# Mixer outputs of a two-layer encoder trunk: gated projections by seven half-size products, weight sums by accumulating transfers

## The chip, the cores and the metric

The kernel runs on one core of one Trainium2 chip. The metric is the device time of one execution in microseconds. Each time is the median of several runs of the same program; one more execution is recorded by the hardware profiler, and its trace has its own time. Engines: PE (TensorE) multiplies matrices, DVE (VectorE) and ACT (ScalarE) do elementwise work, POOL (GpSimd) issues some DMAs and does small elementwise work, SP (SyncE) issues the weight loads.

## The reference

Two layers over 640 tokens (512 of a prompt and 8 x 16 of running streams) with a width of 1024:

```python
x += 0.5 * swiglu_1(rmsnorm(x))
z = rmsnorm(x) @ w_in            # columns: B | C | V | q | k | v | gates (2 x 1024)
g_conv, g_attn = split(sigmoid(z_gates + b_gate))
y_conv = B * causal_depthwise_conv3(C * V)          # 512 channels
y_attn = chunk_band_attention(q, k, v)              # 8 heads x 64
m = g_conv * (y_conv @ w_conv_out) + g_attn * (y_attn @ w_attn_out)
x += m @ w_o
x += 0.5 * swiglu_2(rmsnorm(x))
```

All data are fp32. The change is in the line that computes m: `y_conv @ w_conv_out` and `y_attn @ w_attn_out`, each 512 channels in and 1024 columns out, each result multiplied by its gate, the two summed.

## The kernel before, in words

**Layout.** Activations are kept transposed: tiles of 128 channels by 640 tokens. x has 8 such tiles, y_conv and y_attn 4 each, the mixture m 8 ("mixtures" below are these tiles, m_0 to m_7). Tokens fall into two halves of 320, written t1 and t2.

**Precision.** Each fp32 operand is split into a high part (rounded to the fp32r format, a cast on ACT) and a low part (operand minus high part, a subtraction on DVE). A product is three matmuls of 128 x 128 weights with 320 tokens: high x high, high x low, low x high. So every slab of weights costs an ACT cast (whi) and a DVE subtraction (wlo).

**Weights.** All weights lie in HBM in the order of their use, in slabs of 128 x 1024 (512 KB). SP loads them into a ring of three raw tiles (`load`, L275). `source` (L293) says which columns make up the next piece, `prep` (L334) casts it on ACT and notes the subtraction, `flush` (L350) issues noted subtractions on DVE, `slab` (L357) takes the next piece and prepares the piece after the next, `quiet` (L378) takes one without preparing, and `ahead` (L370) issues the load and sums of a piece in advance.

**Plain products and products by seven.** A plain product of one output tile is 4 input tiles x 2 token halves x 3 = 24 matmuls (`product`, L432; for the output products of w_o it is 8 input tiles, 48 matmuls). Most of the kernel computes two output tiles at a time by seven products in place of eight: the 2 x 2 blocks are (output tile, token half) by (even and odd input tile). A unit takes two slabs of weights, from which four pieces of 1024 columns (the last of 512) are made by sums on DVE (four adds of 512 columns, two of which can be replaced by lent sums, below), and seven mixed operands of the inputs, called X11, X21, N6, T5, T7, X22, T4. Each of the seven is a block of 12 matmuls (`block`, L436), in the order of their names. X11, N6, T7 and T4 accumulate one after the other in accumulator pa, X21 in pb, T5 and X22 in pc. ACT copies pa out after X11 (to c1) and after N6 (to u2), and pc after T5 (to c5), before the next block goes on in the same accumulator. DVE adds these copies to the results.

**Stage around the change.** `outputs` (L1469) runs after attention. Its engines' order is the order in which the code issues instructions (PE, DVE and ACT; POOL and SP are ordered by a scheduler). `gate_pair` (L1479) computes two tiles of gates by seven, 84 matmuls, and applies the sigmoid (L1334) at its end. `out` (L1522) computes one projection tile by a plain product (accumulator py, one of two) and multiplies it by its gate (L1530, L1532), for the attention branch adding it to the mixture. The order is given by `mixer_order` (L114): gates 2 and 3, projections 0 to 3 of y_conv, then six times a pair of gates followed by two projections. `take` (L1538) splits y into parts ahead of its products, `give` (L1542) splits the finished mixtures m_0 to m_7, which take the place of the normed input in memory (tiles hhi and hlo). After that come the eight output products po of `mixer` (about L1408 to L1418), each over all eight mixtures, added to x.

**Lent sums.** In the FFN the seven-product units on the list LEAN get one weight sum not from DVE but from two DMAs on POOL's queue: the first copies 128 x 512 weights into a tile, the second adds other weights onto it (`lend`, L268; transfers L272 and L273). The second waits for the first. In the mixers there are none.

Of the kernel before, what the change touches and what calls it, by code (L numbers as in the profile page):

```python
# [57 lines left out]
ROWS = (1, 2)  # L58

MARGIN = 2, 4  # L60
LEAN = {"a0": (1, 6), "b0": (1, 5), "a1": (0, 5), "b1": (1, 5)}

XT4, XN6, XT7, X21, X22, X11, XT5 = range(7)
# [64 lines left out]


# [6 lines left out]
def stages():  # L136

    out, done = [], []

    def end(kind):  # L140
        done.append((kind, out[:]))
        out.clear()

    def plain(n):
        out.extend([8] * (n // 8) + [n % 8] * (n % 8 > 0))

    def ffn(name):
        held = 0
        for what, a in ffn_order(name):
            if what == "gu":  # L150
                plain(held)
                held = 0
                out.append("gu")
            elif what == "std":
                held += 2 * KT
            elif what == "cut":
                plain(held)
                held = 0
            elif what == "rows":
                plain(held)  # L160
                held = 0
                out.append("gu")
            elif what == "ends":
                held += KT * len(a)
            else:
                held += sum(len(js) for _, js in a)
        plain(held)

    for l in range(L):
        ffn(f"a{l}")  # L170
        end("ffn")
        held = 0
        for what, _ in mixer_order():
            if what == "mix":
# [12 lines left out]
def two(ps):  # L187
    return ps[:, :, :HT]
# [7 lines left out]
def trunk(ctx: ExitStack, tc: tile.TileContext, xin, wst, small, pbias, samplebias, kcache, vcache, gfin,  # L196
# [54 lines left out]
    for kind, units in stages():  # L251
        n = sum(2 if z in ("gu", "mix") else 1 for z in units)
        if kind == "ffn":
            inner.update(range(at + MARGIN[0], at + n - MARGIN[1]))
        at += n
    raws, ready = [], []
    sums, pool, spool = {}, [None], [None]
    lent, lean, at = {}, set(), 0
    for name, (_, units) in zip([f"{k}{l}" for l in range(L) for k in "amb"], stages()):
        ns = []  # L260
        for z in units:
            if z == "gu":
                ns.append(at)
            at += 2 if z in ("gu", "mix") else 1
        if name in LEAN:
            lean.update(ns[slice(*LEAN[name])])
# [26 lines left out]
    def source(i):  # L293

        if i >= len(slabs):
            return None
        if i not in sources:
            kind, n, arg = slabs[i]
            ra = load(n)
            if kind == "plain":  # L300
                sources[i] = [(ra, slice(0, arg))]
            elif arg == 0:
                if n in lean and n not in lent:
                    lend(n)
                sources[i] = [(ra, whole)]
            else:
                rb = load(n + 1)
                if arg == 1 and kind == "gu":
                    if n + 2 in lean:
                        lend(n + 2)  # L310
                    st = sums[n] = pool[0].tile([P, CH], F32, tag="s65", name=f"s65_{n}", bufs=1)
                    add(st[:, h2], rb[:, h1], rb[:, h2])
                    add(st[:, h1], st[:, h2], ra[:, h1])
                    sources[i] = [(st, whole)]
                elif arg == 1:

                    flush()
                    st = sums[n] = spool[0].tile([P, CH // 2], F32, tag="s6", name=f"s6_{n}", bufs=1)
                    add(ra[:, h1], ra[:, h1], rb[:, h1])
                    add(st, ra[:, h1], rb[:, h2])  # L320
                    add(rb[:, h1], rb[:, h1], rb[:, h2])
                    sources[i] = [(st, h1), (rb, h1)]
                elif arg == 2:
                    if kind == "gu" and n not in lean:
                        add(ra[:, h1], ra[:, h1], rb[:, h1])
                    add(ra[:, h2], sums.pop(n)[:, h1], ra[:, h2])
                    sources[i] = [(lent.pop(n), h1), (ra, h2)] if n in lean else [(ra, whole)]
                else:
                    sources[i] = [(rb, h2)]
        return sources[i]  # L330

    pending = []
# [984 lines left out]
    def mixer(l, after):  # L1317
        with tc.tile_pool(name=f"yp{l}", bufs=1, reuse_waits="tile") as yp, \
# [84 lines left out]
            with tc.tile_pool(name=f"gp{l}", bufs=1, reuse_waits="tile") as gp, \  # L1403
                 tc.manual_schedule(engines=ORDERED):
                hold[0] = True
                mo = outputs(l, gp, ops.X, st, cs, ycs, yas, sigmoid, gates)
        ex = after()
        with tc.manual_schedule(engines=ORDERED):  # L1408
            hold[0] = True
            for m in range(KT):  # L1410
                po = acc(f"po{l}_{m}")
                product(po, mo)
# [53 lines left out]
        def t5(self, kp):  # L1466
            self.parts(*(z[:, HT:] for z in self.h[2 * kp]), self.a[kp][:, 1])

    def outputs(l, gp, X, st, cs, ycs, yas, sigmoid, gates):  # L1469
# [4 lines left out]
        mm = ycs + [spare[i // 2][:, i % 2] for i in range(CT)]  # L1474
# [4 lines left out]
        def gate_pair(m, then=None):  # L1479
# [5 lines left out]
            ACT.copy(c1, pa)  # L1485
# [7 lines left out]
            ACT.copy(u2, pa)  # L1493
            block(pc, s1, 1, XT5, every, True, True)
            ACT.copy(c5, pc)
            s2 = slab(True)[0]
# [5 lines left out]
            if then:  # L1502
                then()
            block(pc, s2, 1, X22, every, False, True)
            add(u[:, t2], pc, u2)
            s3 = slab(True)[0]
            DVE.tensor_tensor(out=u, in0=u, in1=rr, op=ALU.mult)
# [6 lines left out]
            sigmoid(g, m + 1, -1.0)  # L1514
            flush()

        def parts(pool, tag, name, src):
# [3 lines left out]

        def out(m, y, then=None):  # L1522

            py = acc(f"py{l}_{m}")
            product(py, y)
            if then:
# [7 lines left out]
            flush()  # L1534

        yc, ya, mo = [], [], []

        def take(y, name, srcs):  # L1538
            for c, src in enumerate(srcs):
                y.append(parts(gp, f"y{c}", f"{name}{l}_{c}", src))  # L1540
# [5 lines left out]
        gate_pair(2, lambda: take(yc, "yc", ycs))  # L1546
        for m in range(4):
            out(m, yc)
        for m in range(4, 2 * KT, 2):
            last = m == 2 * KT - 2  # L1550
            gate_pair(m, (lambda: take(ya, "ya", [yas[:, c, :] for c in range(CT)])) if m == KT else
                      (lambda: give(range(1))) if last else None)
            y = yc if m < KT else ya
            out(m, y, (lambda: give(range(1, 4))) if last else None)
            out(m + 1, y, (lambda: give(range(4, 6))) if last else None)
        give(range(6, KT))
        return mo

    def attention(l, h, norms, stats, ops, mp, yas, ycp, both, others):
# [517 lines left out]
def _stream(i):  # L2077
# [9 lines left out]
    for l in range(L):  # L2087
# [36 lines left out]
        for what, m in mixer_order():  # L2124
            if what == "v":
                out.append(v.reshape(KT // 2, 2, P, AW).transpose(0, 2, 1, 3).reshape(-1, P, CH))
            elif what == "mix":
                out.append(chunks(held))
                held = []

                out.append(chunks([rows[name][a][o::2] for name, a in m for o in range(2)]))
            else:
                held.append(rows[what][m])
        out.append(chunks(held))
# [71 lines left out]
```

## Time and profile before

| | |
|---|---|
| median of 3 runs | 2489.51 us (2488.77 to 2489.75) |
| the profiled execution's own time | 2488.93 us |
| span in its trace | 2487.1 us |
| mean granted TensorE clock | 0.999 |
| weight loads on SP | 375 of 512 KB |
| lent sums on POOL | 36 transfers of 256 KB |

In the page and the views of the trace, "busy" counts the time in which an engine has an instruction running. Matmuls overlap, so a matmul's duration is not what it costs; the distance between starts is. Instructions of DVE and ACT overlap a little too. A group line gives the operation, the tiles written and read, the shapes, the count, busy time and mean duration in ns, and then the idle time of the engine before these instructions with what ended it. A timeline line gives start, duration, engine, line, operation, tiles, and in brackets the idle time before it. A window line gives, for a stretch of the span, the busy time of each engine with its instructions, the granted clock, the busy share of the DMA engines and GB/s.

### The profile page before, as it was taken

Reading aid. Unit: us, or ns where it says so; the run is one execution under the profiler, and the core shown is the slowest. Engines: PE = TensorE matmul, PEld = TensorE weight load, DVE = VectorE, ACT = ScalarE, POOL = GpSimd, SP = SyncE. Lnnn points to the kernel's source line nnn. Section 1 sums busy time; section 2 is a strip of 40 time slices with the busy share of each in tenths; the row PEclk is TensorE's granted clock in tenths of the full one; section 3 lists DMA queues with packets and bytes.
Section 4 is the critical chain, followed back from the end, with each engine's and each line's share of the span. In section 5 each row is a group of like instructions: output and inputs, shape, how many; then the busy total and the mean of one; then the engine's idle time right before and its main releaser. Section 6 shows DMA issues by size and latency. Waiting matters only on the chain.

```text
span 2487.1 us, 43918 instructions
## 1 busy us (share of the span) xinstructions
PE 2473.8 (99%) x17312; PEld 2421.2 (97%) x17312; DVE 2140.1 (86%) x3533; ACT 1355.4 (54%) x2152; POOL 298.4 (12%) x451
## 2 busy tenths in 40 slices
PE   9999999999999999999999999999999999999999
PEld 8999999889999999999999999998999999999998
DVE  7999998888776899998799999988886769999997
ACT  6555556665444655555665555556644455555555
POOL 0111112211000001111001011121110000111111
PEclk9999999999999999999999999999999999999999
DMA  4443545335223333444334443453442232444444
GB/s 155 126 118 101 124 118 121 113 108 174 77 82 114 93 102 105 113 117 117 111 93 109 110 118 101 116 128 106 133 157 86 77 111 87 109 116 105 113 117 117
DMA packets 109934, 279.75 MB, mean 112 GB/s; under 512 B 12480, under 2 KB 52032, under 8 KB 109728
## 3 DMA queue, kind: packets, MB, share of 16 engines
q1 hardware_dynamic: 69552, 220.10, 28.0%
q0 software_dynamic: 39744, 56.60, 12.3%
q8 instruction: 135, 2.21, 0.4%
q14 instruction: 71, 0.58, 0.1%
q10 hardware_dynamic: 432, 0.25, 0.0%
HBM read 231.09 MB, written 7.94 MB: 96 GB/s over the span
## 4 chain that ended last, share of the span: by engine, by line
PE 94%; DVE 3%; ACT 2%; issue 1%; DMA 1%; SPq 0%; DVEq 0%; ACTq 0%; POOLq 0%
PE pab L442 12%; PE paa L442 11%; PE pcb L442 6%; PE daa L1127 6%; PE pca L442 5%; PE dab L1127 5%; PE po L418 5%; PE py L418 5%; PE qa L442 4%; PE pbb L442 3%; PE dca L1127 3%; PE pba L442 3%; PE dcb L1127 2%; PE ma_cv L442 2%; PE ma_qk L442 2%; PE pv L1612 2%
## 5 line engine op out<-in xcount | busy, mean ns | idle before, releaser
L352 DVE TENSOR_TENSOR wlo<-raw,whi 128x1024 fp32r<-128x1024 f32 (+1 forms) x569 | 579.9, 1021 | 155.9 <-ACT whi L347 152.8
L347 ACT CAST whi<-raw 128x1024 fp32r<-128x1024 f32 (+1 forms) x569 | 504.7, 890 | 380.1 <-PE pbb L442 47.2
L347 ACT CAST whi<-s 128x1024 fp32r<-128x1024 f32 (+1 forms) x158 | 150.3, 951 | 296.1 <-issue 111.2
L442 PE MATMUL pab<-xhib,whi 128*128 128x320 f32 x704 | 217.7, 309 | 0.0
L442 PE MATMUL pab<-xhib,wlo 128*128 128x320 f32 x704 | 217.3, 309 | 0.0
L442 PE MATMUL pab<-xlob,whi 128*128 128x320 f32 x704 | 217.3, 309 | 0.0
L442 PE MATMUL paa<-xhia,whi 128*128 128x320 f32 x640 | 197.8, 309 | 0.2 <-DVE ga L287 0.2
L442 PE MATMUL paa<-xhia,wlo 128*128 128x320 f32 x640 | 197.6, 309 | 0.0
L442 PE MATMUL paa<-xloa,whi 128*128 128x320 f32 x640 | 197.5, 309 | 0.0
L352 DVE TENSOR_TENSOR wlo<-s,whi 128x1024 fp32r<-128x1024 f32 (+1 forms) x158 | 173.5, 1098 | 4.6 <-ACT whi L347 4.6
L1149 POOL DMA_DIRECT2D x<-c_a x80 | 70.2, 1030 | 574.1 <-ACT ahia L1031 205.4
L442 PEld LDWEIGHTS pab<-xhib,whi 128*128 128x128 f32 x704 | 132.2, 188 | 0.9 <-issue 0.9
L1149 POOL DMA_DIRECT2D x<-c_b x72 | 63.2, 1013 | 582.0 <-ACT ahib L1031 205.6
L442 PEld LDWEIGHTS pab<-xlob,whi 128*128 128x128 f32 x704 | 132.2, 188 | 0.0
L442 PEld LDWEIGHTS pab<-xhib,wlo 128*128 128x128 f32 x704 | 132.2, 188 | 0.0
L442 PEld LDWEIGHTS paa<-xhia,whi 128*128 128x128 f32 x640 | 120.1, 188 | 1.1 <-DVE ga L287 0.5
L442 PEld LDWEIGHTS paa<-xloa,whi 128*128 128x128 f32 x640 | 120.2, 188 | 0.3 <-DVE xloa L686 0.3
L442 PEld LDWEIGHTS paa<-xhia,wlo 128*128 128x128 f32 x640 | 120.1, 188 | 0.2
L442 PE MATMUL pcb<-xhib,wlo 128*128 128x320 f32 x352 | 108.9, 309 | 0.0
L442 PE MATMUL pcb<-xlob,whi 128*128 128x320 f32 x352 | 108.6, 309 | 0.0
L442 PE MATMUL pcb<-xhib,whi 128*128 128x320 f32 x352 | 108.6, 309 | 0.0
L287 DVE TENSOR_TENSOR raw<-s,raw 128x512 f32<-128x512 f32 x158 | 107.9, 683 | 0.0
(764 smaller groups left out, 8077.7 us busy)
## 6 DMA issues: line engine op xcount, KB each, us to landing
raw<-in_wst SPq DMA_DIRECT2D x375, 512.0 KB, 3.6
x<-c_a POOLq DMA_DIRECT2D x80, 160.0 KB, 4.7
x<-c_b POOLq DMA_DIRECT2D x72, 160.0 KB, 3.6
lent<-in_wst POOLq DMA_DIRECT2D x36, 256.0 KB, 3.9
kc<-in_kcache SPq DMA_DIRECT2D x32, 256.0 KB, 4.9
vc<-in_vcache SPq DMA_DIRECT2D x16, 512.0 KB, 4.9
x<-u_a POOLq DMA_DIRECT2D x40, 160.0 KB, 3.9
x<-u_b POOLq DMA_DIRECT2D x36, 160.0 KB, 3.9
```

What stands on the lines that cost most here:

```text
L287: DVE.tensor_tensor(out=out, in0=a, in1=b, op=op)
L347: ACT.copy(hi[:, d], src[:, c])
L352: DVE.tensor_tensor(out=lo, in0=src, in1=hi.bitcast(F32), op=ALU.subtract)
L418: PE.matmul(ps[:, a, :HT], w, x[a] if isinstance(x, tuple) else x[:, a * HT : (a + 1) * HT], start=first and j == 0 and not seeded, stop=l ...
L442: PE.matmul(ps, a, b, start=start and kp == 0 and j == 0, stop=stop and kp == NP - 1 and j == 2, skip_group_check=True)
L1127: PE.matmul(ps[u], w, y, start=start and i == 0 and j == 0, stop=i == 1 and j == 2, skip_group_check=True)
L1149: POOL.dma_start(x[ms[2 * u + r]][:, cols], z[:, u], accum_op=ALU.add)
L1612: PE.matmul(pv[t], xx[:, t * P : (t + 1) * P], w[:, kk * AW : (kk + 1) * AW], start=c == 0 and kk == 0 and j == 0, stop=c == KT // 2 - 1 a ...
```

## The change

Three quarters of the gated projections (y_conv to tiles 4 to 7, y_attn to tiles 0 to 3 and 4 to 7) are computed four tiles at a time by seven products, in a unit called rows (84 matmuls over two slabs of weights, in place of 4 x 24). The first four tiles of y_conv remain plain.

- The stage's order becomes: gates 2, plain co 0 to 3, gates 4, gates 6, rows co(4-7), gates 8, gates 10, rows ao(0-3), gates 12, gates 14, rows ao(4-7), output products.
- The seven mixed operands of y_conv and y_attn are made by DVE (sums and differences, in place) and split by ACT and DVE, in steps (`mixed`) spread over the plain products and gate pairs.
- The sigmoids of a gate pair are issued one unit later, after its first ACT copy (`due`). The results of rows co are copied from the gate tiles to the mixture tiles by ACT at the same place in gates 8; the attention branch is added to the mixtures by DVE (`total`) in gates 12 and 14 and at the end.
- Nine units a layer (gates 4 to 14 and the three rows) have two weight sums made by accumulating DMAs on POOL's queue, in tiles "three" and "one" of which there is one buffer each: four transfers of 256 KB a unit. The first for unit n + 1 is issued with the third piece of unit n, the other three with its fourth.
- Mixtures m_0 to m_3 are split inside gates 14 (m_0 and m_1 after the first block, m_2 and m_3 after T7); m_4 to m_7 after the last rows unit.
- The first two output products are interleaved: both go over mixtures 0 to 3, then each over 4 to 7.

```diff
@@ mixer_order
-    out += gates[:2] + [("co", m) for m in range(4)]
-    for i, g in enumerate(gates[2:]):
-        name, m = ("co", 4 + 2 * i) if i < 2 else ("ao", 2 * i - 4)
-        out += [g, (name, m), (name, m + 1)]
+    out += gates[:2] + [("co", m) for m in range(4)] + gates[2:4] + [("rows", ("co", (4, 5, 6, 7)))]
+    for i in range(2):
+        out += gates[4 + 2 * i : 6 + 2 * i] + [("rows", ("ao", tuple(range(4 * i, 4 * i + 4))))]
@@ lent sums
+    def lend_part(n, tag, second=False):
+        k, c = {"three": ((n + 1, h1), (n + 1, h2)), "one": ((n, h1), (n + 1, h1))}[tag][second]
+        if not second:
+            lent[n, tag] = apart[0].tile([P, CH // 2], F32, tag=tag, name=f"{tag}{n}", bufs=1)
+        POOL.dma_start(lent[n, tag], wst[k][:, c], **({"accum_op": ALU.add} if second else {}))
+    def lend_rest(n):
+        for tag, second in (("one", False), ("three", True), ("one", True)):
+            lend_part(n, tag, second)
@@ source
+                elif arg == 1 and n in lean:
+                    three = lent.pop((n, "three"))
+                    st = sums[n] = spool[0].tile([P, CH // 2], F32, tag="s6", name=f"s6_{n}", bufs=1)
+                    add(st, three, ra[:, h1])
+                    sources[i] = [(st, h1), (three, h1)]
...
+                if arg > 1 and kind == "mix" and n in lean and after_mix[n] in lean:
+                    lend_part(after_mix[n], "three") if arg == 2 else lend_rest(after_mix[n])
@@ output products
+            first = [acc(f"po{l}_{m}") for m in range(2)]
+            ws = [[tiles.take() for _ in mo] for _ in first]
+            for ks in (range(KT // 2), range(KT // 2, KT)):
+                for p, w in zip(first, ws):
+                    for k in ks:
+                        multiply(p, w[k], mo[k], k == 0, k == KT - 1)
@@ gate_pair
             ACT.copy(c1, pa)
+            due()
             prep(used[0] + 1)
             flush()
+            at[0]()
             block(pb, s0, 1, X21, every, True, True)
...
-            sigmoid(u, m)
+            lates.append(lambda: sigmoid(u, m))
@@ new in outputs
+        def mixed(i, y, z):
+            z = z.rearrange("p c (a b) -> p (c a) b", a=2)
+            e1, e2, o1, o2 = (z[:, i] for i in range(4))
+            add(e1, e1, e2, ALU.subtract)
+            add(e2, o2, e2, ALU.subtract)
+            for out, a in ((o2, e1), (o1, o2)):
+                DVE.scalar_tensor_tensor(out=out, in0=a, scalar=-1.0, in1=out, op0=ALU.mult, op1=ALU.subtract)
+            yield
+            hi, lo = (gp.tile([P, 3, HT], F32R, tag=f"x{i}{p}", name=f"x{p}{l}_{len(more)}") for p in ("hi", "lo"))
+            ACT.copy(hi, z[:, 1:])
+            more.append((hi, lo))
+            yield
+            low(lo, z[:, 1:], hi)
+            yield
+            hi, lo = (u[:, t2] for u in y[2 * i])
+            ACT.copy(hi, e1)
+            yield
+            low(lo, e1, hi)
+            yield
...
+        def rows(name, ms, y):
...
+            w = quiet()
+            mul(a, w, 0, X11, True)
+            ACT.copy(s1, two(A))
+            due()
+            prep(used[0] + 1)
+            flush()
+            mul(b, w, 1, X21, True)
+            add(s1, two(B), s1)
+            w = slab(True)[0]
+            flush()
+            mul(a, w, 0, XN6, False)
+            ACT.copy(s2, two(A))
+            gated(0, [s1[:, u] for u in range(2)], t1)
+            mul(c, w, 1, XT5, True)
+            for u in range(2):
+                ACT.copy(s5[:, u], c[u])
+            w = slab(True)[0]
+            mul(a, w, 0, XT7, False)
+            add(s5, two(A), s5)
+            flush()
+            ahead()
+            gated(1, [s5[:, u] for u in range(2)], t2, -1.0)
+            mul(c, w, 1, X22, False)
+            for u in range(2):
+                add(s2[:, u], c[u], s2[:, u])
+            w = slab(True)[0]
+            gated(0, [s2[:, u] for u in range(2)], t2)
+            mul(a, w, 0, XT4, False)
+            flush()
+            gated(1, a, t1, -1.0)
+            if name == "co":
+                lates.append(lambda: [ACT.copy(mm[m], g) for m, g in zip(ms, gs)])
...
+        gate_pair(2, [none, none, lambda: take(yc, "yc", range(CT), ycs)])
+        z = [mixed(i, yc, ycp[i]) for i in range(2)]
+        out(0, yc, going(z[0]))
+        out(1, yc, also(going(z[0]), going(z[1])))
+        out(2, yc, also(going(z[0]), going(z[1])))
+        out(3, yc, going(z[1]))
+        both = also(going(z[0]), going(z[1]))
+        gate_pair(4, [both, none, both])
+        gate_pair(6, [none] * 3)
+        rows("co", (4, 5, 6, 7), yc)
+        z = [mixed(i, ya, yas[:, 2 * i : 2 * i + 2]) for i in range(2)]
+        pair = lambda c: (take_even(c, yas_[c]), take(ya, "ya", [c + 1], yas_))
+        go = [going(u) for u in z]
+        gate_pair(8, [lambda: pair(0), lambda: pair(2), go[0]])
+        gate_pair(10, [also(go[0], go[1]), also(go[0], go[1], go[0]), also(go[1], go[0], go[1], go[1])])
+        rows("ao", (0, 1, 2, 3), ya)
+        gate_pair(12, [lambda: total(0, 2), none, lambda: total(2, 4)])
+        gate_pair(14, [lambda: give(range(2)), none, lambda: give(range(2, 4))])
+        rows("ao", (4, 5, 6, 7), ya)
+        for m in range(4, KT):
+            total(m, m + 1)
+            give([m])
```

More of the change, by code (lines that the diff above doesn't have):

```diff
@@ L255, in trunk @@
         at += n
+    mixes = [n for kind, n, arg in slabs if kind == "mix" and arg == 0]
+    apart = [None]
+    after_mix = dict(zip(mixes, mixes[1:] + [None]))
     raws, ready = [], []
@@ L1477, in outputs, with due, gate_pair @@
         every = range(NP)
[L1479 removed]
+        lates = []
+        def due():
+            for f in lates:
+                f()
+            lates.clear()
+        def gate_pair(m, at):
             n = f"{l}_{m}"
@@ L1536, in outputs, with take @@
         yc, ya, mo = [], [], []
-        def take(y, name, srcs):
-            for c, src in enumerate(srcs):
-                y.append(parts(gp, f"y{c}", f"{name}{l}_{c}", src))
+        more = []
+        yas_ = [yas[:, c, :] for c in range(CT)]
+        def take(y, name, cs, srcs):
+            for c in cs:
+                y.append(parts(gp, f"y{c}", f"{name}{l}_{c}", srcs[c]))
         def give(ms):
@@ L1556, in outputs, with low @@
-        give(range(6, KT))
+        def low(lo, z, hi):
+            DVE.tensor_tensor(out=lo, in0=z, in1=hi.bitcast(F32), op=ALU.subtract)
+        def mixed(i, y, z):
[17 more added lines that the diff above has]
+            yield
@@ new lines, in take_even, with kind @@
+        def take_even(c, src):
+            y = tuple(gp.tile([P, T], F32R, tag=f"y{c}{i}", name=f"ya{l}_{c}{i}") for i in ("hi", "lo"))
+            split(*(z[:, t1] for z in y), src[:, t1])
+            ya.append(y)
+        EXTRA = XT7, XT4, XN6
+        def kind(y, i, k):
+            if k in EXTRA:
+                return tuple(z[:, EXTRA.index(k)] for z in more[i - 2])
+            hi, lo = y[2 * i + (k in (X21, X22))]
+            return tuple(z[:, t2 if k in (X22, XT5) else t1] for z in (hi, lo))
@@ new lines, in total, with also, going @@
+        def total(m0, m1):
+            for m in range(m0, m1):
+                add(mm[m], mm[m], gates[KT + m])
+        none = lambda: None
+        def also(*fs):
+            return lambda: [f() for f in fs]
+        def going(z):
+            return lambda: next(z)
+        gate_pair(2, [none, none, lambda: take(yc, "yc", range(CT), ycs)])
[3 more added lines that the diff above has]
+        out(2, yc, also(going(z[0]), going(z[1])))
@@ L2131, in _stream @@
                 out.append(chunks([rows[name][a][o::2] for name, a in m for o in range(2)]))
+            elif what == "rows":
+                out.append(chunks(held))
+                held = []
+                name, ms = m
+                out.append(chunks([rows[name][a][o::2] for r in range(2) for o in range(2)
+                                   for a in ms[2 * r : 2 * r + 2]]))
             else:
```

72 lines of the change are left out of this document (48 added, 24 removed).

## The prediction

> **What bounds the kernel now.** I read the page's head first, then its chain, then windows inside the stage that changes, then PE's waits.
>
> ```profile
> span 2487.1 us, 43918 instructions
> ...
> PE 2473.8 (99%) x17312; PEld 2421.2 (97%) x17312; DVE 2140.1 (86%) x3533; ACT 1355.4 (54%) x2152; POOL 298.4 (12%) x451
> ...
> PE 94%; DVE 3%; ACT 2%; issue 1%; DMA 1%; SPq 0%; DVEq 0%; ACTq 0%; POOLq 0%
> ```
>
> PE is busy 2473.8 of 2487.1 us and makes up 94% of the chain: whatever takes a matmul away shortens the kernel, if nothing else makes PE wait. The changed stage runs at about 635 to 778 us in layer 0 and again in layer 1. The first window below is one gate pair of it (84 matmuls), the second a stretch of the first FFN.
>
> ```profile
> core 0: us, PE busy (x) PEld busy (x) DVE busy (x) ACT busy (x) POOL busy (x), PEclk, DMA share, GB/s
> 681.16:693.47 12.31, 12.31 (x87) 12.31 (x86) 6.84 (x10) 4.84 (x7) 0.00 (x0) 1.00 0.29 89
> 200.00:300.00 100.00, 100.00 (x684) 100.00 (x683) 92.53 (x146) 52.82 (x77) 14.10 (x16) 1.00 0.47 117
> ```
>
> In the gate pair PE never stops, DVE works 6.84 of 12.31 us, ACT 4.84, POOL not at all. So there is room beside PE here. The FFN shows that PE can stay at 100% with DVE at 92.5%.
>
> PE's waits in the whole run, longest first, and what PE's output products waited for:
>
> ```profile
> PE poa L418 <- ACT whi L742: 5.5, 1, 5.5
> PE pca L442 <- DVE wlo L352: 0.5, 2, 0.3
> ```
> ```profile
>   DVE m_6lo L235: 0.3, 2
> ```
>
> The longest is the start of the kernel. The changed stage loses 0.3 us in two places, where the output products wait for the seventh mixture. There is no stall to win back: the gain can only be matmuls.
>
> **What it removes.** Of the 16 plain products per layer (24 matmuls each), 12 become three units of 84 matmuls: 288 become 252, so 36 fewer per layer and 72 in all. The instruction lists agree: 16778 matmuls before, 16706 after. What one costs is not its duration of 0.31 us, because they overlap. It is the distance from the first matmul of a gate pair to the first one after it:
>
> ```profile
> 681.16 0.31 PE L442 MATMUL qa<-hhim,whi 128*128 128x320 f32 x1
> ...
> 693.46 0.46 PE L418 MATMUL py<-yc_0hi,whi 128*128 128x320 f32 x2
> ```
>
> (693.46 - 681.16) / 84 = 0.1464 us, and 72 x 0.1464 = **10.5 us saved**. The wait of 0.3 us is replaced by another, below.
>
> [...]
>
> **What it adds beside PE.** DVE durations by shape, then how closely instructions follow each other on DVE and on ACT:
>
> ```profile
> L352 DVE TENSOR_TENSOR wlo<-raw,whi 128x1024 fp32r<-128x1024 f32 x357 | 435.9, 1221 | 155.9 <-ACT whi L347 152.8
> ...
> L352 DVE TENSOR_TENSOR wlo<-raw,whi 128x512 fp32r<-128x512 f32 x212 | 144.8, 685 | 0.0
> ...
> L686 DVE TENSOR_TENSOR xlob<-xob,xhib 128x960 fp32r<-128x960 f32 x8 | 9.2, 1154 | 0.7 <-ACT xhib L617 0.7
> ...
> L287 DVE TENSOR_TENSOR g<-qc,capsm 128x320 f32<-128x320 f32 x14 | 6.8, 484 | 0.0
> ```
> ```profile
> 711.62 0.81 DVE L235 TENSOR_TENSOR ya_0lo<-ya,ya_0hi 128x640 fp32r<-128x640 f32 x1
> 712.36 0.82 DVE L235 TENSOR_TENSOR ya_1lo<-ya,ya_1hi 128x640 fp32r<-128x640 f32 x1
> ```
> ```profile
> 683.11 0.43 ACT L1485 COPY capsm<-qa 128x320 f32<-128x320 f32 x1 [4.46 <-PE qa L442]
> 683.43 1.05 ACT L347 CAST whi<-raw 128x1024 fp32r<-128x1024 f32 x1
> ...
> 693.66 1.55 ACT L1334 ACTIVATE g<-g,sm 128x640 f32<-128x640 f32 x2 [0.86 <-DVE g L1507]
> ```
> ```profile
> 774.15 0.72 ACT L234 CAST m_1hi<-yc 128x640 fp32r<-128x640 f32 x1
> 774.78 0.72 ACT L234 CAST m_2hi<-yc 128x640 fp32r<-128x640 f32 x1
> ```
>
> A DVE instruction costs its duration less about 0.08 us (640 columns: 0.74 apart): 1.14, 0.60, 1.07 and 0.40 us for 1024, 512, 960 and 320. On ACT a 640 cast or copy costs 0.63, a 320 copy 0.32, a sigmoid 0.75, a 512 cast about 0.53 (between those two by width). ACT starts 0.19 us after PE ends: 681.16 + 12 x 0.1464 = 682.92 against 683.11.
>
> With these I summed DVE's instruction list of the changed kernel (layer 0) by unit; PE needs 12.3 us for each: gate 4 8.9, gate 6 8.1, rows co 10.9, gate 8 12.0, gate 10 12.7, rows ao(0-3) 10.9, gate 12 11.1, gate 14 11.1, rows ao(4-7) 10.2. From 8 to the last this is 68.0 of 73.8 us, 92%: like the FFN. So DVE does not become the bound by its sum; what is late is late by order. I walked the queues through each unit, its blocks of 12 matmuls (1.76 us) being X11, X21, N6, T5, T7, X22, T4. T7 goes on in the accumulator that ACT copies to u2 after N6, so T7 (7.03 us into the unit) waits for ACT. The sigmoids move behind the next unit's first copy, 1.5 us of ACT there; ACT's idle half covers that, except where more stands with them.
>
> - Plain products 2 and 3 reuse the accumulators of 0 and 1, whose multiplication now stands behind four DVE mixtures (1.7 us): **0.25 us** a layer.
> - Gate 8: behind the first copy (2.27) ACT has four copies of finished products (2.5), two 512 casts (1.06), a 320 and a 640 cast (0.95), one more 512 cast (0.53) and the copy to u2 (0.43), which ends at 7.75: T7 waits **0.75 us**.
> - Gate 10: after T7's result at 9.0 DVE has 6.2 us of work (two of the four mixtures among it), so it ends 3.0 to 3.6 us into the rows unit, and the low weights for N6 (needed at 3.8) come up to 0.5 us late: **0.5 us**.
> - Gate 14: the first two mixtures are cast before X21 is issued, but into tiles of normed input that T5 reads last. ACT waits for them until 5.9, casts twice (7.15), casts weights (7.7), copies u2 (8.1): **1.0 us**.
> - The handover to the output products is the largest. After the last T4, DVE still has gates and weights to do (from T7's result at 9.0: 0.8 add, 1.14, 0.8, 0.8, 0.8, 1.14, 0.8), ending at 15.3, and then four times in a row a sum, a cast on ACT and a low part. Before, the same three steps follow each other without a gap:
>
> ```profile
> 782.18 0.83 DVE L287 TENSOR_TENSOR mm<-mm,g 128x640 f32<-128x640 f32 x1
> ...
> 783.80 0.83 DVE L235 TENSOR_TENSOR m_7lo<-mm,m_7hi 128x640 fp32r<-128x640 f32 x1
> ```
> ```profile
> 783.04 0.73 ACT L234 CAST m_7hi<-mm 128x640 fp32r<-128x640 f32 x1 [3.47 <-DVE mm L287]
> ```
>
>   That is 2.35 us a mixture (0.86 + 0.76 + 0.74). With the first low part done at 17.9, the last ends at 25.0. PE covers 12.3 + 7.0 us with the first four mixtures of two products, and would be through the eighth mixture of the first product at 22.9; it gets there at 25.7: **2.8 us**.
>
> Together 5.3 us a layer, 10.6 us in both layers.
>
> **The transfers.** Nine units a layer get two weight sums by accumulating DMAs on POOL's queue, 4 x 256 KB a unit, instead of two of DVE's four 512 adds (1.2 us). The nearest rows are the FFN's sums, first and second transfer, then the queues:
>
> ```profile
> DMA to landing us min/median/max: 3.0/3.6/5.7
> ```
> ```profile
> DMA to landing us min/median/max: 3.6/4.0/7.3
> ```
> ```profile
> q1 hardware_dynamic: 69552, 220.10, 28.0%
> q0 software_dynamic: 39744, 56.60, 12.3%
> ```
>
> The second waits for the first, and the first for DVE's last read of the one buffer. So a pair takes 7.6 us at the medians, 6.6 to 13.0 at the ends. DVE comes back to the sum 7 to 9 us after freeing the buffer, so it is just in time. But at 5.4 us per MB (0.123 x 2487.1 / 56.60) 1.05 MB adds 5.7 us of all engines to each 12.3 us: the DMA share goes from 0.29 to about 0.75, and landings get longer. I take 0.4 us more per pair, nearer to the medians than to the maxima, passed on by three or four late units a layer: 1.4 us, **2.8 us** in both. POOL had nothing else to do here; SP issues as many DMAs as before (467 in both instruction lists).
>
> [...]
>
> **Sum.** The profiled execution took 2488.93 us. - 10.5 - 0.3 + 10.6 + 2.8 = + 2.6, so 2491.5. The median of the runs, 2489.51, lies 0.6 above it: **2492 us**, within what a measurement of this kernel can tell from no change (about 0.2%, 5 us).
>
> **Rivals.**
> - *Hidden after all.* The DVE sum and the FFN window (PE 100% with DVE at 92.5%) speak for it: stalls shrink when a late unit is followed by a light one. If only the handover stays, 2489.5 - 10.8 + 5.6 = 2484; if that is hidden too, 2479. Against it stand ACT's queue in gates 8 and 14 and the handover, where order and not load decides. Chance 0.2.
> - *The transfer loop takes over (slower).* Buffer freed, two landings, sum, cast, the unit's last gating (u, rr, g: 1.7 us), low parts (1.2), buffer freed: 7.6 + 0.6 + 1.7 + 1.2 = 11.1, plus what stands between in gates 8, 10, 12 and 14 (1.5 to 1.9): up to 13.0 us against PE's 12.3. From a pair of about 8 us on, every further us is paid in five units a layer: a pair of 9 costs about 5 us a layer, so 2488.9 - 10.8 + 10.6 + 10 + 0.6 = 2499. POOL's in-order queue and the single buffer speak for it, the medians against. Chance 0.3.
> - *The products aren't saved.* Excluded by the matmul counts; PEclk is 1.00 in the windows, so nothing there changes the 0.146.
>
> **How the numbers follow.** Forecast (2487 to 2496) 0.5, hidden 0.2, loop 0.3. Faster by over 0.2% (under 2484.5) holds most of the hidden case: 0.17. Slower (over 2494.5) is the loop and the upper edge of the forecast, 0.08: 0.38. The rest, 0.45, is within 0.2%. The range 2482 to 2501 leaves out the case with a hidden handover and a pair of over 9 us, about 0.1 on each side.
>
> **What would show it.** The matmul distance of 0.146 again; PE waits that name ACT's u2 copy in gates 8 and 14; waits of the output products for m_6lo and m_7lo of about 1 us each, 2.8 in sum per layer; DVE's weight sum waiting for a DMA seldom and briefly. Against the loop: landings of 3.6 and 4.0 as before. If PE waits in the stage sum to under 3 us a layer, the queue walk was wrong; if DVE's sums wait over 1 us for transfers in most units, the transfers were under-priced.

## The result, and the profile after

Median of the changed kernel: 2520.93 us (2517.24 to 2524.9, 4 runs), against 2489.18 (2488.77 to 2489.75) before: ratio 1.0128, 95% interval 1.0116 to 1.0141. It is 31.7 us slower; 2492 had been forecast, with 2501 as the upper end. The profiled execution took 2522.16 us.

The page's head and chain of the changed kernel:

```profile
span 2520.4 us, 44096 instructions
...
PE 2481.5 (98%) x17240; PEld 2419.9 (96%) x17240; DVE 2182.5 (87%) x3653; ACT 1390.9 (55%) x2236; POOL 348.9 (14%) x523
...
PE 82%; DVE 6%; DMA 5%; issue 5%; ACT 2%; POOL 0%; SPq 0%; DVEq 0%; POOLq 0%; ACTq 0%
```

17240 matmuls instead of 17312: the 72 are gone. Yet PE's share of the chain fell from 94% to 82%, and that of DMAs rose from 1% to 5%. PE's waits of the whole run (total, times, longest):

```profile
PE qa L466 <- DVE wlo L376: 6.9, 6, 1.7
...
PE raao L1647 <- ACT capsm L1661: 4.9, 2, 3.2
PE qa L466 <- ACT capsm L1538: 4.8, 4, 1.8
PE qa L466 <- ACT capsm L1528: 3.3, 3, 1.6
PE po L442 <- ACT m_7hi L234: 1.3, 2, 0.6
PE po L442 <- ACT m_6hi L234: 1.2, 2, 0.6
```

The names are DVE and ACT, but both wait for something themselves. DVE's timeline in layer 0, the weight sum of each unit (time, duration, and in brackets the idle time before it and what ended it):

```profile
688.56 0.69 DVE L300 TENSOR_TENSOR s<-three,raw 128x512 f32<-128x512 f32 x1 [2.18 <-DMA three<-in_wst]
...
701.89 0.69 DVE L300 TENSOR_TENSOR s<-three,raw 128x512 f32<-128x512 f32 x1 [3.00 <-DMA three<-in_wst]
...
716.97 0.69 DVE L300 TENSOR_TENSOR s<-three,raw 128x512 f32<-128x512 f32 x1 [1.80 <-DMA three<-in_wst]
...
732.44 0.69 DVE L300 TENSOR_TENSOR s<-three,raw 128x512 f32<-128x512 f32 x1 [1.84 <-DMA three<-in_wst]
...
747.63 0.69 DVE L300 TENSOR_TENSOR s<-three,raw 128x512 f32<-128x512 f32 x1 [1.45 <-DMA three<-in_wst]
...
763.02 0.69 DVE L300 TENSOR_TENSOR s<-three,raw 128x512 f32<-128x512 f32 x1 [3.78 <-DMA three<-in_wst]
```

Six sums in a row wait for their transfer and follow each other every 14.9 us ((763.02 - 688.56) / 5), where PE needs 12.3 us a unit. What makes 14.9 is on POOL's timeline:

```profile
706.62 0.57 POOL L282 DMA_DIRECT2D three<-in_wst  x1 [2.91 <-DVE g L1656]
710.50 0.86 POOL L282 DMA_DIRECT2D three<-in_wst  x1 [3.30 <-DMA three<-in_wst]
711.04 0.89 POOL L282 DMA_DIRECT2D one<-in_wst  x1
718.09 0.86 POOL L282 DMA_DIRECT2D one<-in_wst  x1 [6.16 <-DMA one<-in_wst]
722.80 0.57 POOL L282 DMA_DIRECT2D three<-in_wst  x1 [3.85 <-DVE wlo L376]
```

The first transfer into three takes 3.9 us (706.62 to 710.50), the accumulating one 6.5 (to the sum at 716.97), and 5.8 us pass until DVE has read three for the last time and POOL starts the next (722.80). That is a circle of 16.2 us through one buffer. In the six pairs started from 678.65 to 752.30 the two transfers took 9.4 to 10.7 us, the rest 3.9 to 5.8.

ACT passes the delay on. Its queue, and then PE's:

```profile
763.82 0.62 ACT L371 CAST whi<-s 128x512 fp32r<-128x512 f32 x1 [7.54 <-DVE s L300]
764.35 0.61 ACT L371 CAST whi<-three 128x512 fp32r<-128x512 f32 x1
764.87 0.42 ACT L1528 COPY capsm<-qa 128x320 f32<-128x320 f32 x1
```
```profile
765.34 0.42 PE L466 MATMUL qa<-thi,whi 128*128 128x320 f32 x1 [1.41 <-ACT capsm L1528]
```

The copy of X11's result has nothing to do with the transfer. It stands behind two casts that wait for the sum (ACT idle 7.54 us), and PE waits for the copy.

The third loss is no wait at all. Windows around one stall (the column after POOL is the granted clock):

```profile
734.50:738.00 3.50, 1.37 (x7) 0.97 (x6) 3.46 (x8) 2.39 (x4) 0.00 (x0) 0.96 0.00 0
738.00:741.10 3.10, 3.10 (x13) 3.10 (x13) 3.03 (x5) 2.20 (x4) 1.14 (x2) 0.50 0.38 100
741.20:745.70 4.50, 4.50 (x32) 4.50 (x32) 2.27 (x4) 1.80 (x3) 1.79 (x2) 1.00 0.98 308
```

After 3.5 us in which PE worked 1.37, its clock is 0.50. In the 3.1 us of the second line PE is busy all the time, but starts 13 matmuls where 21 fit at 0.1464. That costs 1.2 us more, and PE's busy time rose (2473.8 to 2481.5) with 72 matmuls fewer. Layer 0 has three such stretches (from 737.7, 768.4 and 802.5).

In layer 0, gate 2 to the end of the output products takes 215.4 us (635.66 to 851.08) against 199.2 before: 5.3 saved and 21.5 lost, 3.7 of them in the output products. From the first of the six sums to the last, five units take 74.5 us instead of 61.5: this pace is 13.0 of the 17.7 us lost ahead of the output products (one stretch of low clock lies within it).

### The profile page after: what moved, and what is told of

Same layout as the page of the kernel before. It is cut to its first block, busy times and chain, and to the rows that moved or that the text cites. A ratio compares the mean times of both kernels' runs of the same rounds, so it can differ in the third digit from the quotient of the medians.

```text
span 2520.4 us, 44096 instructions
## 1 busy us (share of the span) xinstructions
PE 2481.5 (98%) x17240; PEld 2419.9 (96%) x17240; DVE 2182.5 (87%) x3653; ACT 1390.9 (55%) x2236; POOL 348.9 (14%) x523
## 4 chain that ended last, share of the span: by engine, by line
PE 82%; DVE 6%; DMA 5%; issue 5%; ACT 2%; POOL 0%; SPq 0%; DVEq 0%; POOLq 0%; ACTq 0%
PE pab L466 12%; PE paa L466 11%; PE pcb L466 6%; PE daa L1151 6%; PE pca L466 5%; PE dab L1151 5%; PE po L442 4%; DMA three<-in_wst 4%; PE pbb L466 3%; PE dca L1151 3%; PE pba L466 3%; PE dcb L1151 2%; PE ma_cv L466 2%; PE ma_qk L466 2%; PE pv L1781 2%
## 5 line engine op out<-in xcount | busy, mean ns | idle before, releaser
L371 ACT CAST whi<-raw 128x1024 fp32r<-128x1024 f32 (+1 forms) x563 | 492.4, 879 | 368.5 <-PE pbb L466 45.5
L376 DVE TENSOR_TENSOR wlo<-raw,whi 128x1024 fp32r<-128x1024 f32 (+1 forms) x563 | 566.0, 1007 | 136.1 <-ACT whi L371 132.2
```

The lines of the kernel that those rows point to most:

```text
L371: ACT.copy(hi[:, d], src[:, c])
L376: DVE.tensor_tensor(out=lo, in0=src, in1=hi.bitcast(F32), op=ALU.subtract)
```

## The experiments

My theory: the circle through the single buffer of three is the bound, and ACT's and DVE's queues carry its delay to PE. Rival A: the order of ACT's and DVE's work stalls PE, whatever the transfers do. Others: DVE itself (B), the transfers' traffic (C), the buffer of one (D), and, where the order is mended, that each wait removed lets another of its size appear (A2).

**Sums back on VectorE.** No mixer unit gets transfers:

```
-        lean.update(ns[slice(*LEAN.get(name, (FREE, None)))])
+        if name in LEAN:
+            lean.update(ns[slice(*LEAN[name])])
```

> The changed kernel with its mixer weight sums back on VectorE, as the kernel before makes them: no transfer into three or one, two more 512-column sums (0.60 us each between starts) a unit. Theory (the transfer loop is the bound): no sum waits for a DMA any more, the ACT casts and the copies behind them come in time, and most of the stage's stalls of 17.7 us a layer go. VectorE then has 11 units of 12.3 us and nine of them with 1.2 us more, so gates 8 and 10 pass 12.3 us by about 1 us each; with that, 0.7 at gate 14 and 3.7 at the handover a layer, minus 5.3 saved: about 2491 us, 2485 to 2499. Rival A (the order of the ACT and VectorE work stalls TensorE whatever the transfers do): 2510 us or more, the stalls at gates 8, 10, 14 and at the rows stay. Rival B (VectorE without the transfers is the bound in its turn): 2500 to 2515 us, with TensorE waiting for wlo in most units.

Measured: 2515.40 us, ratio 1.0104 [1.0089, 1.0119]. The theory's number failed. The time is 0.4 us above B's range; it lies in A's too, so this run alone doesn't separate the two. The window over gates 8 to 14, that of gates 8 and 10 alone, and two of DVE's waits there:

```profile
700.00:790.00 90.00, 80.95 (x520) 77.54 (x519) 80.18 (x133) 48.16 (x76) 0.00 (x0) 0.98 0.24 75
700.60:730.57 29.97, 25.84 (x170) 24.67 (x169) 27.01 (x48) 18.12 (x30) 0.00 (x0) 1.00 0.22 72
```
```profile
707.74 1.23 DVE L377 TENSOR_TENSOR wlo<-raw,whi 128x1024 fp32r<-128x1024 f32 x1 [1.37 <-ACT whi L372]
...
722.98 1.23 DVE L377 TENSOR_TENSOR wlo<-raw,whi 128x1024 fp32r<-128x1024 f32 x1 [1.17 <-ACT whi L372]
```

DVE works 80.2 of the 90 us, and in these two waits it stands for the cast of a sum that it has just made: a sum on DVE costs 0.6 us, and here a wait of 1.2 to 1.4 besides. Gates 8 and 10 take 30.0 us together (700.60 to 730.57) for 24.6, and DVE has 27.0 us of work in them. So DVE does need help there; the run doesn't tell whether the transfers hurt.

**One sum, two buffers.** Only one is transferred, with the room of three as its second buffer:

```
-            lent[n, tag] = apart[0].tile(..., bufs=1)
+            lent[n, tag] = apart[0].tile(..., bufs=2)
...
+                    add(rb[:, h1], rb[:, h1], rb[:, h2])
+                    add(st, rb[:, h1], ra[:, h1])
...
+                if arg == 3 and kind == "mix" and n in lean and after_mix[n] in lean:
+                    lend_one(after_mix[after_mix[n]])
```

> The changed kernel with one of the two transferred sums a unit (one) instead of two; the 2 KB of three make a second buffer for it, so that each pair of transfers starts two units ahead, and VectorE makes three itself. Theory (the loop on one buffer is the bound): a pair of 9 us has 24.6 us, no sum and no cast waits for a DMA, VectorE has 0.6 us more a unit. The stalls left are 0.7 at gate 14, some 1 at gates 8 and 10 and 3.7 at the handover a layer, minus 5.3 saved: about 2488 us, 2483 to 2495. Rival A (order): 2510 or more. Rival C (it is the traffic of the transfers, not the waiting for a buffer, that costs): about half of the changed kernel's loss stays, 2504 to 2512.

Measured: 2498.94, ratio 1.0039 [1.0024, 1.0054]. Below A and C, 4 us above the theory's range; no sum or cast waits for a transfer into one. With DVE doing one sum more than in the changed kernel, 22 us come back.

**The transfers in the kernel before.** Both sums, on single buffers, at gates 4 to 14, the products left as they were.

> The kernel before, with both transferred sums on single buffers added at gates 4 to 14 and nothing else changed: its units are a gate pair and two plain products, 19.3 us. Theory (the loop costs only where a unit is shorter than it, 14 to 16 us as traced): no wait, 2489 us, within 2 us of the kernel before. Rival C (the transfers' traffic costs by itself, wherever it is): TensorE or the sums wait here too, 2494 us or more.

Measured: 2489.22, ratio 1.0000 [0.9990, 1.0010]: the theory, and against C. From issue to landing the transfers into one took:

```profile
DMA to landing us min/median/max: 3.7/5.8/8.0
```

Longer than in the changed kernel (3.3/4.9/6.7), and free: a unit here is 19.3 us long. With the longer unit the traffic is thinner too (1.05 MB in 19.3 us instead of 12.3), so the next run but one is the harder test of C.

**The order alone.** Transfers as in the changed kernel:

```
-        gate_pair(14, [lambda: give(range(2)), none, lambda: give(range(2, 4))])
+        gate_pair(14, [none, none, lambda: give(range(4))])
         rows("ao", (4, 5, 6, 7), ya)
-        for m in range(4, KT):
-            total(m, m + 1)
-            give([m])
+        total(4, KT)
+        give(range(4, KT))
```

> The changed kernel with its transfers, but two orders altered: the last four mixtures are all summed before the first is cast, and the casts of the first four stand late in gate 14 and not at its start. Theory (the transfer loop is the bound): the handover's waits of 2.5 to 3.7 us a layer go, the stalls at gates 8 to 14 and at the rows stay: 2512 to 2516 us. Rival A (order is the main cause): most of the loss goes, below 2500 us.

Measured: 2519.61, ratio 1.0122 [1.0106, 1.0137]. A is out. The theory expected 5 to 9 us of gain, and 1.3 came: the output products come to 56.3 us (before 56.6), but the stretch ahead of them grows by 1.3 us in layer 0 and 1.7 in layer 1. In layer 0 gate 14 and the rows unit behind it take 32.3 us together (30.5 in the changed kernel): most of what the order gave was lost again ahead of it.

**A second buffer for three alone**, the same bytes moved (the room comes from letting the third staging tile of the row products share the first; three's pair is now issued a unit earlier):

```
-            lent[n, tag] = apart[0].tile(..., bufs=1)
+            lent[n, tag] = apart[0].tile(..., bufs=2 if tag == "three" else 1)
```

> The changed kernel with all its transfers, and a second buffer for three: that sum is started two units ahead instead of one (the room comes from letting the third staging tile of the row products share the first). The same bytes move as in the changed kernel. Theory (the loop on one buffer is the bound; the sums in three were what VectorE waited for in 6 of 8 units): no sum waits for three any more, VectorE has 87% and less than 12.3 us in most units; the stalls that are left are those of the order (about 1 at gate 8, 1 at gate 14, 0.8 in the plain products, 3.7 at the handover a layer): 2489 us, 2485 to 2495. Rival C (the traffic of four transfers a unit costs, not the waiting for a buffer): 2508 us or more. Rival D (the other sum, one, on its single buffer takes over as the loop): waits of whi for one of 1 us or more in most units, 2500 to 2512.

Measured: 2497.03, ratio 1.0033 [1.0022, 1.0044]: 24 us from one buffer, at unchanged traffic, so C (2508 or more) is out. DVE waits for three no more. The time is 2 us above the theory's range; a small part is D, ACT waiting for one (in the whole run):

```profile
ACT whi L382 <- DMA one<-in_wst: 3.6, 4, 1.2
```

**Two buffers and the order mended in four places**, first on three, then on one alone. Beside the two edits above, the first row unit writes its products straight into the mixtures (no ACT copies at gate 8), and `then()` in the plain products stands behind their multiplication.

> The kernel of the second buffer for three, and the order mended in four places: the last four mixtures are summed before the first is cast; the casts of the first four mixtures stand late in gate 14; the products of the first row unit are written straight to the mixtures, so that the four ACT copies at the head of gate 8 go; the mixing step in the plain products stands behind the product's own evacuation. Theory: of the stalls a layer the handover's 3.7, gate 14's 1, gate 8's 1 and the plain products' 0.8 go, and the 10.5 us of saved products show: 2480 us, 2478 to 2485, below the kernel before. Rival A2 (the order's stalls hide others of nearly the same size behind them): 2486 to 2490, no better than before.

> The kernel with one transferred sum a unit on two buffers, and the same four places of order mended. Theory: from 2498.9 us, the handover's 4.1 and 3.7 go, with 1.2 each at gates 8 and 14 a layer, and 0.8 a layer in the plain products; left are the stalls of gate 10 and of the row products behind it, where VectorE has 13.3 to 14 us for 12.3: about 2486 us, 2483 to 2490. Rival B (VectorE is the bound as soon as it makes one of the two sums itself): 2492 or more.

Measured: 2486.69, ratio 0.9992 [0.9983, 1.0001], and 2489.99, ratio 1.0004 [0.9995, 1.0013]. On single buffers two of these edits gave 1 us; here the four give 10 and 9. The first result is A2's, not the theory's: other waits (low weights at the attention rows 0.5 each, u2 at gate 8 0.9) stayed or came, and ACT's waits for one grew from 3.6 to 9.6 us. The second is at the theory's upper end.

**Four buffers**, with a further mended order and with the order untouched:

> The changed kernel with two buffers for both transferred sums (three and one), each pair started two units ahead, with the order mended as in the run of two buffers for three, and two steps put later on VectorE: two of the four casts of gate 14 and the last two low halves of the mixed attention rows now stand in the row unit behind. Theory: the casts that still waited for one (5.6 us of ACT in a layer, 0.4 to 0.9 us of TensorE at gates 6 and 8) go, and so do the waits of 0.5 us for the low weights in the two attention row units; of 2486.7 us some 6 go: 2480 us, 2478 to 2484. Rival C (more transfers at once are slower, so that a second buffer only makes the same traffic queue): 2486 or more, sums waiting for three again. Rival A2 (other waits of the order take their place): 2484 to 2488.

> The changed kernel with two buffers for both transferred sums and no order mended. Theory (loop first, order second): from 2497.0 us with two buffers for three alone, the waits for one go, 2 to 4 us: 2494 us, 2490 to 2497; what is left above the kernel before is the order's: handover 4.1 and 3.7, gate 8 about 0.7, gate 14 about 1, plain products 0.8 a layer, minus 5.3. Rival C (traffic): 2497 or more.

Measured: 2488.37, ratio 0.9998 [0.9989, 1.0007], and 2497.42, ratio 1.0031 [1.0018, 1.0044]. Both expectations failed: neither is better than with one buffer for one, and both times lie above the lower bound that C had set (2486 and 2497). Sums don't wait for three or one again, though, as C supposed. Mended waits were replaced, one of them at the start of the stage, on DVE's timeline of the first kernel:

```profile
635.43 0.69 DVE L302 TENSOR_TENSOR raw<-raw,raw 128x512 f32<-128x512 f32 x1 [2.22 <-DMA raw<-in_wst]
```

Two pairs of transfers now start at once and delay a plain slab by 2.2 us; gate 2 starts 1.0 and 1.6 us late. This is the one place found where traffic itself cost, as C had it. The other new wait: copies behind two casts that I had put at the head of a row unit, 1.9 us a layer.

The second kernel shows what the change's order costs without the circle, by PE's waits in the whole run behind its start (this execution took 2501.2 us, the longest of five):

```profile
PE qa L468 <- ACT ya L2003: 4.6, 2, 2.6
PE qa L468 <- ACT capsm L1541: 3.3, 4, 1.0
PE po L444 <- ACT m_7hi L234: 1.3, 2, 0.6
PE po L444 <- ACT m_6hi L234: 1.2, 2, 0.6
PE raao L1650 <- DVE wlo L378: 1.0, 2, 0.5
```

The first row is the late start of gate 2 (2.0 and 2.6 us here), more than the 3.6 us that ACT had waited for one; the others are gates 8 and 14, the handover and the attention rows.

**Four buffers, second and third order.** The second pair of transfers waits for gate 2's first copy, the sigmoids in the row units stand behind the copies of N6, and the casts of the first four mixtures are moved twice:

```
+        def second():
+            POOL.tensor_copy(go2, cs[0][:, :1])
+            lend_both(after_mix[first])
...
-        gate_pair(14, [none, none, lambda: give(range(2))])
-        rows("ao", (4, 5, 6, 7), ya, none, lambda: give(range(2, 4)))
+        gate_pair(14, [none, lambda: give([0]), lambda: give([1, 2])])
+        rows("ao", (4, 5, 6, 7), ya, lambda: give([3]))
```

> The run of four buffers with the order mended, with three things more: the second pair of transfers waits for the first copy of gate 2 instead of starting with the first pair (there, the raw slab for gate 2's successor landed 2.2 us late and gate 2 began 1.0 and 1.6 us late); two of the four casts of the mixtures stand in the middle of the last row unit and not at its head; in the row units the gates' sigmoids stand behind the copies of N6, whose lateness held TensorE 1.9 us in each layer. Theory: from 2488.4 us these 1.3 and 2.7 us a layer go (3.2 in rows, 0.1 to 0.2 of restart at each): 2481 us, 2478 to 2485, below the kernel before by 0.2 to 0.4 per cent. Rival A2 (the next wait in the queue takes the place of each one removed): 2485 to 2490.

> The run before it (four buffers, second order), with the four casts of the first mixtures spread over the pauses that its trace shows on VectorE: one in the middle of gate 14 (idle 2.2 us there), two at its end, one at the start of the last row unit, none in that unit's middle. Theory: the wait of 1.0 us at the handover, for VectorE's last products of that unit, goes in both layers: 2482.3 us, 2480.5 to 2484. Rival A2 (another wait takes its place): 2484 or more.

Measured: 2484.42, ratio 0.9982 [0.9973, 0.9991], and 2482.34, ratio 0.9974 [0.9963, 0.9984], both inside the theory's range. The last is faster than both kernels, by 6.6 us than the one before. PE's waits in its whole run, and a window of it:

```profile
PE poa L444 <- ACT whi L768: 5.7, 1, 5.7
PE qa L468 <- ACT ya L2006: 0.7, 2, 0.4
PE raao L1654 <- ACT rs L1679: 0.5, 2, 0.3
```
```profile
680.00:700.00 20.00, 20.00 (x138) 20.00 (x137) 14.87 (x26) 10.32 (x19) 5.22 (x7) 1.00 0.75 203
```

Behind the start of the kernel nothing over 0.7 us is left, and PE runs at full clock with the DMA share at 0.75.

**The fourth corner**: that order, on single buffers and with the transfers started as in the changed kernel.

> The mended order of the fastest run (casts, mixtures, row products, plain products), but with the changed kernel's single buffer for each transferred sum and its start of the transfers: the fourth corner of order by buffers. Theory (the loop sets the length of a unit, whatever stands in the order: 14 to 15 us as traced in the changed kernel for units of 12.3): the order buys only what lies outside the loop, the handover's 2.7 to 3.7 and the plain products' 0.8 a layer: 2510 to 2516 us. Rival A (order is the main cause, the buffers only help): below 2500 us.

Measured: 2518.68, ratio 1.0120 [1.0103, 1.0137], 3 us above the theory's range and far from A. DVE's waits for three, in the whole run, here and (second) in the changed kernel:

```profile
DVE s L300 <- DMA three<-in_wst: 36.9, 14, 4.0
```
```profile
DVE s L300 <- DMA three<-in_wst: 28.7, 11, 4.0
```

So the four corners are:

| us | single buffers | two each |
|---|---|---|
| order of the change | 2520.9 | 2497.4 |
| order mended | 2518.7 | 2482.3 |

And the units of layer 0, from PE's first matmul of each to that of the next:

| us | gate 4 | gate 6 | rows co | gate 8 | gate 10 | rows ao | gate 12 | gate 14 | rows ao |
|---|---|---|---|---|---|---|---|---|---|
| changed kernel | 12.3 | 12.3 | 12.7 | 16.1 | 14.7 | 16.5 | 12.8 | 18.2 | 12.3 |
| two buffers each | 12.3 | 12.3 | 12.3 | 13.2 | 12.8 | 13.1 | 12.3 | 13.5 | 12.3 |
| and order mended | 12.3 | 12.3 | 12.3 | 12.3 | 13.1 | 12.9 | 12.3 | 12.3 | 12.5 |

## Why the prediction was wrong

- **10.5 us of matmuls saved: right.** The blocks of 12 matmuls keep 1.76 us, and in the fastest kernel gate 2 to the output products takes 138.9 us instead of 142.7, 3.8 of the 5.3 a layer. In the changed kernel the saving was more than used up: from gate 8 to gate 14 PE was no longer what set the pace.
- **DVE isn't the bound by its sum: right** with the transfers (87% of the span). The first run shows the other side, which I had not worked out: without them its work in gates 8 and 10 (27.0 us) is longer than PE's (24.6).
- **Stalls by order, 5.3 us a layer: the places right, the sizes too small.** With two buffers each and the order untouched, layer 0 loses 0.8 in the plain products (14.91 us for 14.08; forecast 0.25), 0.9 at gate 8 (0.75), 1.2 at gate 10 and the rows behind it (0.5), 1.2 at gate 14 (1.0) and 3.7 at the handover (60.29 for 56.56; 2.8): about 8, a half more. Part of the handover's excess is a lower clock (matmuls 0.27 us apart from 793.0 to 794.6, and a mean of 0.97 from 780 to 842).
- **The transfers: the step that failed**, "I take 0.4 us more per pair, [...] passed on by three or four late units a layer: 1.4 us". The pair was taken as 8.0 us and measured 9.4 to 10.7. The second transfer was mis-sized most: 5.8 to 6.9 us, from issue to the sum, for 4.0. One's first transfer is issued within 0.5 to 2.4 us of it and SP's slabs run beside both, while the 4.0 came from a stage that lends one sum a unit, not two; that this is why, is read, not tried. The time from the sum to the last read (3.5 to 5.4 in my loop) was right: 3.9 to 5.8. So the circle is 13.8 to 16.2 us, over PE's 12.3 in each of the six, and in the trace six units of layer 0 and five of layer 1 were late, by 1.5 to 4.0 us each at the sum. Priced at 2.8 us, the single buffers cost 23.5 with the order as it was (2520.9 against 2497.4).
- **The rival "transfer loop takes over" was the mechanism**, with its decisive point (a pair of about 8 us) and its direction. Its price of 2499 supposed a pair of 9, and a delay that PE pays once a unit; by its own rule a pair of 10 gives 2509, an estimate still 12 us short. In the trace the late sum also holds ACT's queue (idle 7.54 us ahead of 763.82), and with it copies that PE needs at the same place in every gate; two stalls then come close together. The sign I had set, "if DVE's sums wait over 1 us for transfers in most units", is what the trace shows: 11 of 18 do, 28.7 us in all.
- **"Landings of 3.6 and 4.0 as before": not for one.** Three's took 3.0 to 7.5 us, 3.7 in the middle, and one's 3.3 to 6.7, 4.9 in the middle. None was under 3.0 us, though that occurs at this size: in the trace of before the ten stores of 256 KB from POOL's queue (out_vo) landed in 2.3 to 3.5 us, 2.6 in the middle.
- **"Nothing there changes the 0.146": wrong.** Behind stalls the clock fell to 0.50 and the distance rose to 0.267 us, six times in the changed kernel; the kernel before shows no such stretch up to 2480 us, and the fastest one none in its windows from 640 to 820 us (clock 1.00 in each).
- **The terms don't add.** I summed order and transfers. Mending the order is worth 2 us on single buffers and 15 on two (up to 4 of these by the later start of the second pair of transfers); the buffers are worth 23.5 and 36. Together they are worth 38.6 us (2520.9 to 2482.3), where the two singly give 2.2 and 23.5: each hid part of what the other costs.

How much of the 17.7 us that layer 0 loses ahead of the output products is the circle's delay, and how much the clock's, wasn't separated by a run; by the windows the clock's part there is two stretches of about 1.2 us. No run thinned the traffic in these units while keeping the single buffers, so why the second transfer is longer stays open.

## What to carry to other kernels

Compare the whole circle of a buffer that transfers fill (both transfers at the lengths of *that* traffic, plus the time until its last reader is through) with the unit it serves. Here the same pairs of transfers were free in units of 19.3 us (2489.22 us, ratio 1.0000) and the bound in units of 12.3 (circles of 13.8 to 16.2 us), and a second buffer took 24 of the 31.7 us away at the same traffic. A late operand cost more than its own reader here (PE waited 1.41 us for a copy that stood behind two casts on ACT): look what stands behind the waiting instruction in each engine's queue. Order and buffering are to be mended together: here the mended order showed 2 us alone and 15 with the second buffers.

## What the hardware showed beside

After close stalls PE's clock fell to 0.50, as in the window from 738.00 to 741.10, its matmuls then 0.267 us apart instead of 0.146. The six drops of this trace begin at 737.7, 768.4, 802.5, 1959.7, 1987.0 and 2017.7 us and last 3.4 us each. In the 3.4 us ahead of each PE was busy 1.2 to 2.1 us.

Not every stall was followed by one. The longest gaps of layer 0's stage, 2.08 us before 710.90 and 2.02 before 721.96, were not; two stalls in 3.5 us with 1.37 us of work were, and so was layer 1's longest, 3.55 us before 1985.34. The 3.4 us that hold most of the two long gaps had 2.13 us of work (707.0 to 710.4) and 2.04 (720.6 to 724.0), about as much as the 2.05 ahead of the drop at 802.5. No sharp limit comes out of these figures, and no run shows what decides.

The four runs of the changed kernel had mean clocks of 0.995 to 0.998 and differ by 7.7 us, those of the fastest kernel 0.999 to 1.000 and 1.9 us; the lower clock is the likely reason, though only read, not tried.
